# Gate/up and w_down of a hybrid encoder layer by seven block products instead of eight

## The chip, the cores and the metric

The kernel runs on one core of one Trainium2 chip. The metric is the device time of one execution in microseconds (us), as the median of several runs. In the profile PE is the tensor engine (TensorE), PEld its weight loads, DVE the vector engine (VectorE), ACT the scalar engine (ScalarE), POOL the GpSimd engine, SP the engine that only issues DMA transfers. TensorE has two clock levels, 1.2 and 2.4 GHz; the column PEclk is the granted share of the full one.

## What is computed

One layer over 512 tokens of width 2048: a token mixer (a gated recurrence beside sparse attention, merged by gates and an output projection), a residual with layer norm, and then the part that changes here:

```python
def swiglu(h, w_gate, w_up, w_down):
    return (jax.nn.silu(h @ w_gate) * (h @ w_up)) @ w_down
...
        h = x * (1.0 + sc_f) + sh_f
        y = swiglu(h, w_gate[l], w_up[l], w_down[l])
        x = layer_norm(ALPHA * x + (1.0 + gt_f) * y, ln2_g[l], ln2_b[l])
```

`w_gate` and `w_up` are 2048 x 5632, `w_down` is 5632 x 2048, all float32.

## The kernel before

Every float32 product runs as three passes in a rounded format: an operand x is split into hi, its rounded copy, and lo = x - hi, and hi*hi + hi*lo + lo*hi is accumulated in PSUM (`mm3`, whose matmuls stand at line 204 of the profile). Activations are feature-major, 128 features on the partitions and 512 tokens along the row, wherever they feed a product; `m_hi` and `m_lo` hold the 16 feature tiles of the normed h.

Weights come as one stream of 128 x 1024 tiles of 512 KB in the order of their use. `Stream.load_to` (line 285) issues the loads on SP into five raw buffers; `round_to` (line 319) rounds a tile to hi on ScalarE, `split_to` (line 331) takes lo on VectorE, into four pairs of buffers. Both run two tiles ahead of the products. The order of instructions on each engine is the order in which the program issues them.

Gate and up (`gate_up`, products at line 204 on tiles `gate` and `up`): for each of 44 feature tiles of 128, gate takes 16 feature tiles of h times three passes, 48 matmuls with all 512 tokens moving, and up as many. ScalarE takes silu of gate out of PSUM (line 1188), VectorE multiplies by up (line 1190), and the result is split (lines 246, 247). The very first feature tile is taken in two halves of 256 tokens while the last two token tiles are still being normed: `finish1` norms a token tile, transposes it (`zt`, line 1096), scales it on ScalarE (line 1103) and splits it on VectorE.

w_down (`down`, tile `dn`): after each part of four feature tiles, for each of four column blocks of 512 and each of four token tiles, 12 matmuls with 128 tokens stationary and 512 weight columns moving. VectorE multiplies each weight tile of w_down by the gate row `gtf` before it is split (line 1022), and adds each PSUM bank into the residual's accumulator (line 1209), which began as ALPHA (z g + b) (`base_side`, on GpSimd). The last part goes token tile by token tile: add (line 1265), statistics (line 1266), `ln_scale`, and `norm` (lines 1272 to 1278), which writes the output.

`Side` holds generators (`finish1`, `base_side`) that are advanced a step between slices of the large products. GpSimd's DMA queue carries the loads of x, of the merge gates and of the layer norm rows.

Of the kernel before, what the change touches and what calls it, by code (L numbers as in the profile page):

```python
# [13 lines left out]
"""  # L14
# [14 lines left out]
P = 128  # L29
# [27 lines left out]
NHEAP = 38  # L57
NSMALL = 14
# [12 lines left out]
def stream_keys():  # L71
    """The weight tiles in the order in which the products use them."""
# [28 lines left out]
    def gu(p):  # L101
        return [(g, f, i) for f in range(p * PART, p * PART + PART) for g in ("gate", "up") for i in range(2)]

    def down(p):
        return [("down", f, c) for c in range(4) for f in range(p * PART, p * PART + PART, 2)]

    ks += gu(0)
    for p in range(1, NPART):
        ks += gu(p) + down(p - 1)
# [3 lines left out]
    ks += [k for k in down(NPART - 1) if not k[2]] + stay  # L113
    return ks
# [3 lines left out]
def layer_kernel(ctx, tc, ws, wa, wada, xt, x, cin, bada, lbl, ghg, gcq, gckv, ln1c, lnrow, ident, lvm, dist, out):  # L118
# [6 lines left out]
    hp = ctx.enter_context(tc.tile_pool(name="heap", bufs=NHEAP))  # L125
# [6 lines left out]

    def big(name, dt=FR):
        return bp.tile([P, 4, T], dt, name=name, tag="big")
# [4 lines left out]
    # ---------------------------------------------------------------- constants  # L139
# [18 lines left out]
    # cond = silu(c) on every partition  # L158
# [64 lines left out]
    keys = stream_keys()  # L223
# [25 lines left out]
    class Stream:  # L249
        def __init__(self):  # L250
# [10 lines left out]
        def room(self, kind):  # L261
            """The pool that an entry is loaded into, and how many of it may be there."""
# [8 lines left out]
        def load_to(self, e):  # L271
            """Load at least up to this entry, and as far as the room reaches."""
            while self.ndma < len(entries):
                kind = entries[self.ndma]
# [1124 lines left out]
```

## Time and profile before

| | |
|---|---|
| median of 3 runs | 2917.91 us (2916.67 to 2919.34) |
| profiled execution, span of its instructions | 2914.7 us |
| what the median of the runs has beyond that span | 3.2 us |
| TensorE busy | 2874.3 us, 99% of the span |
| VectorE, ScalarE, GpSimd busy | 1664.9, 865.0, 382.3 us |
| DMA traffic | 407.46 MB, mean 140 GB/s |

The profiled execution's own time is given by its span alone, so it stands against the runs by their median. The span runs from the first to the last instruction. Engines work side by side, and their busy times are not summed.

### The profile page before, as it was taken

The page shows a single profiled execution, that of the slowest core. Times are in us where ns is not written, and L with a number is a line of the kernel's source. Part 1 is how long each engine was busy: PE and PEld are TensorE (multiplying, and loading weights), DVE is VectorE, ACT ScalarE, POOL GpSimd, SP SyncE. Part 2 cuts the span into 40 slices and gives each one's busy share as a digit, 9 for nine tenths or more (in the row PEclk, how much of TensorE's full clock was granted, in tenths as well). Part 3 has the DMA queues.
Part 4 walks back from the last instruction along what each step waited for, and adds up shares of the span by engine and source line. Part 5 has one row for each costly group of instructions (what it writes and reads, how often), then busy time and mean ns, then how long its engine had stood idle before and what let it go on. Part 6 is the DMA issues. An engine that isn't in the chain of part 4 may idle for free.

```text
span 2914.7 us, 33709 instructions
## 1 busy us (share of the span) xinstructions
PE 2874.3 (99%) x13226; PEld 2391.8 (82%) x13226; DVE 1664.9 (57%) x2429; ACT 865.0 (30%) x1276; POOL 382.3 (13%) x435
## 2 busy tenths in 40 slices
PE   8999999999999999999999999999999999999997
PEld 6878888888888888888888888888888888888885
DVE  7877777778834876456643534244343524344358
ACT  4334342333223554222332222222222222222221
POOL 1011223332012443000062000000000000000003
PEclk9999999999999999999999999999999999999998
DMA  9866455557952124444233322332332233232341
GB/s 387 329 203 190 154 170 175 177 174 261 315 194 95 51 73 169 149 137 130 75 121 101 102 96 92 101 100 88 102 100 96 93 102 99 89 101 97 105 132 65
DMA packets 116049, 407.46 MB, mean 140 GB/s; under 512 B 14225, under 2 KB 14529, under 8 KB 112817
## 3 DMA queue, kind: packets, MB, share of 16 engines
q1 hardware_dynamic: 104690, 369.35, 37.7%
q0 software_dynamic: 10912, 35.64, 3.8%
q8 instruction: 104, 1.70, 0.2%
q14 instruction: 55, 0.45, 0.1%
q10 hardware_dynamic: 288, 0.31, 0.0%
HBM read 386.62 MB, written 16.27 MB: 138 GB/s over the span
## 4 chain that ended last, share of the span: by engine, by line
PE 94%; DVE 3%; DMA 1%; issue 1%; ACT 0%; POOL 0%; SPq 0%; DVEq 0%; POOLq 0%; ACTq 0%
PE gate L204 16%; PE up L204 16%; PE dn L204 16%; PE y L204 6%; PE gb L204 6%; PE ga L204 6%; PE qb L204 3%; PE pb L204 3%; PE g L204 3%; PE v L204 3%; PE pa L204 2%; PE early L204 2%; PE s L204 2%; PE a L204 1%; PE q L204 1%; PE f L204 1%
## 5 line engine op out<-in xcount | busy, mean ns | idle before, releaser
L331 DVE TENSOR_TENSOR wlo<-raw,whi 128x1024 fp32r<-128x1024 f32 (+1 forms) x486 | 597.2, 1251 | 474.4 <-ACT whi L319 470.2
L319 ACT ACTIVATE whi<-raw 128x1024 fp32r<-128x1024 f32 (+1 forms) x486 | 498.7, 1047 | 514.0 <-DVE raw L1022 241.3
L204 PE MATMUL gate<-mhi,wlo 128*128 128x512 f32 (+1 forms) x720 | 276.8, 384 | 0.0
L204 PE MATMUL up<-mhi,wlo 128*128 128x512 f32 (+1 forms) x720 | 276.8, 384 | 0.0
L204 PE MATMUL gate<-mlo,whi 128*128 128x512 f32 (+1 forms) x720 | 276.7, 384 | 0.0
L204 PE MATMUL gate<-mhi,whi 128*128 128x512 f32 (+1 forms) x720 | 276.7, 384 | 0.0
L204 PE MATMUL up<-mlo,whi 128*128 128x512 f32 (+1 forms) x720 | 276.7, 384 | 0.0
L204 PE MATMUL up<-mhi,whi 128*128 128x512 f32 (+1 forms) x720 | 276.7, 384 | 0.0
L204 PE MATMUL dn<-whi,gthi 128*128 128x512 f32 x656 | 255.2, 389 | 0.0
L204 PE MATMUL dn<-wlo,gthi 128*128 128x512 f32 x656 | 255.2, 389 | 0.0
L204 PE MATMUL dn<-whi,gtlo 128*128 128x512 f32 x656 | 255.2, 389 | 0.0
L1209 DVE TENSOR_TENSOR t<-t,dn 128x512 f32<-128x512 f32 x160 | 106.5, 684 | 141.2 <-PE dn L204 140.2
L1190 DVE TENSOR_TENSOR silu<-silu,up 128x512 f32<-128x512 f32 x43 | 29.6, 687 | 271.3 <-PE up L204 271.3
L1253 POOL DMA_DIRECT2D l<-in_lnrow x8 | 4.3, 542 | 1299.0 <-PE dn L204 1212.4
L204 PEld LDWEIGHTS gate<-mlo,whi 128*128 128x128 f32 x720 | 135.3, 188 | 26.9
L204 PEld LDWEIGHTS gate<-mhi,whi 128*128 128x128 f32 x720 | 135.3, 188 | 26.8
L204 PEld LDWEIGHTS up<-mlo,whi 128*128 128x128 f32 x720 | 135.3, 188 | 26.8
L204 PEld LDWEIGHTS up<-mhi,whi 128*128 128x128 f32 x720 | 135.3, 188 | 26.8
L204 PEld LDWEIGHTS gate<-mhi,wlo 128*128 128x128 f32 x720 | 135.3, 188 | 26.8
L204 PEld LDWEIGHTS up<-mhi,wlo 128*128 128x128 f32 x720 | 135.3, 188 | 26.8
L204 PEld LDWEIGHTS dn<-whi,gthi 128*128 128x128 f32 x656 | 123.1, 188 | 25.6
L204 PEld LDWEIGHTS dn<-wlo,gthi 128*128 128x128 f32 x656 | 123.1, 188 | 25.6
(349 smaller groups left out, 5672.2 us busy)
## 6 DMA issues: line engine op xcount, KB each, us to landing
raw<-in_ws SPq DMA_DIRECT2D x480, 512.0 KB, 3.9
raw<-in_wada SPq DMA_DIRECT2D x128, 512.0 KB, 4.9
rawb<-in_wada SPq DMA_DIRECT2D x22, 1024.0 KB, 12.1
raws<-in_wada SPq DMA_DIRECT2D x40, 256.0 KB, 6.3
d_gate<-sgate POOLq DMA_DIRECT2D x32, 256.0 KB, 3.0
raw<-in_wa SPq DMA_DIRECT2D x16, 384.0 KB, 10.0
raws<-in_xt SPq DMA_DIRECT2D x16, 256.0 KB, 10.3
spa<-d_gate POOLq DMA_DIRECT2D x16, 256.0 KB, 3.1
```

The source lines that it names most:

```text
L204: mmul(*a, **k)
L319: nc.scalar.activation(hi, src, AF.Copy)
L331: nc.vector.tensor_sub(lo, src, hi.bitcast(FT))
L1190: nc.vector.tensor_mul(s, s, ps)
L1209: nc.vector.tensor_add(yacc[t][c], yacc[t][c], ps)
L1253: nc.gpsimd.dma_start(rows2[n][c], lnrow[2 + n][:, c * T:c * T + T].to_broadcast([P, T]))
```

## The change

The product of two matrices cut into 2 x 2 blocks is taken by seven block products instead of eight.

For gate and up the blocks of the weights are feature tiles p and p + 22 of the output (the first digit of a block's name) and the two halves of the 2048 input features (the second digit), and h is cut into the same halves of features and into two halves of 256 tokens. A group (`gu`, n) is one pair of feature tiles of gate or up; there are 44, with seven products each (p1, q7, r6, p2, q5, q4, p3). A product takes one 128 x 1024 weight block and eight feature tiles of one 256-token half of h or of a combination of halves: 24 matmuls of 256 columns. The combinations R4 to R7 of h are made once by `block_sums`, after `finish1`. The products accumulate in three PSUM banks per group; the partial sums are copied out by ScalarE and combined by VectorE.

The weights need four sums, S3 = 11 + 21, S1 = 21 + 22, S2 = S1 + 11, S4 = S2 + 12. For all but the first four groups VectorE adds them from the four loaded tiles, between three steps ahead of a group's first product and two steps behind it. For the first four groups (32 transfers, issued during the product with w_pb) and for w_down (176 transfers of 512 KB, issued during gate and up) GpSimd issues DRAM to DRAM transfers, half of them plain copies and half with an add at the destination.

For w_down the blocks are token halves, halves of the 5632 rows and halves of the 2048 columns. `give` forms seven combinations of the activations on VectorE and stores them to DRAM over SP's queue (seven stores of 128 KB for each of 22 pairs); `factor_load` and `factor_tiles` bring them back and split them, eight and four steps ahead. There are 7 x 11 x 2 products of 12 matmuls of 512 columns, summed over all rows in PSUM. The gate row and the base are applied at the end (`join`) and not to each weight tile; the base is formed during the w_down products from normed rows that were spilled to DRAM. The last four products go token tile by token tile.

Weight tiles are still 128 x 1024 in five raw buffers and four pairs, now prepared three steps ahead. The general tile pool of 38 buffers is split after the merge into one of 14 buffers and one of six larger ones; for w_down a pool of 24 stands in the latter's place. The output projection (`y`) keeps its products; its x tiles, the held tiles of w_out and the residual rows (spilled to and read back from DRAM) now pass through the six larger buffers.

The diff, cut to its core:

```diff
+    def block(g, what):
+        if what[0] == "S":
+            return d_sum[g, what]
+        i, j = int(what[0]) - 1, int(what[1]) - 1
+        if g[0] == "gu":
+            return ws[at_row[("gate", "up")[g[1] % 2], g[1] // 2 + i * NP2, j]]
+        return ws[at_row["down", 2 * g[1] + j * NP2, 2 * i + g[2]]]
...
+        return [(g, dst, src, add) for dst, src, add in (
+            ("S3", "11", False), ("S1", "21", False), ("S3", "21", True), ("S1", "22", True),
+            ("S2", "S1", False), ("S2", "11", True), ("S4", "S2", False), ("S4", "12", True)) for g in groups]
+    def add_up(g, dst, src, add):
+        nc.gpsimd.dma_start(d_sum[g, dst], block(g, src), **({"accum_op": OP.add} if add else {}))
+    first_jobs = sum_jobs([("gu", n) for n in range(NPRE)])
+    down_jobs = sum_jobs([("dn", n, cc) for n in range(NP2 // 2) for cc in range(2)])
...
+        for i in ("R7", "R6", "R5", "R4"):
+            raw = {}
+            for t in (0, 1):
+                for c in range(2):
+                    h11, h12, h21, h22 = (hraw.get(at) for at in ((t, c), (t + 2, c), (t, c + 2), (t + 2, c + 2)))
+                    if i == "R7":
+                        raw[t, c] = h22
+                        nc.vector.tensor_sub(h22, h12, h22)
...
+    first = [("gu", n) for n in range(NPRE)]
+    steps = [Unit(first[n], i) for n0 in range(0, NPRE, 2) for i in ("p1", "p2") for n in (n0, n0 + 1)]
+    steps += [Unit(g, i) for i in ("q7", "r6") for g in first]
+    steps += [Unit(g, i) for g in first for i in ("q5", "q4", "p3")]
+    for n in range(NPRE, 2 * NP2):
+        steps += [Unit(("gu", n), i) for i in SEVEN]
+    nsteps = len(steps)
+    steps += [Unit(("dn", n, cc), i) for i in SEVEN for n in range(NP2 // 2) for cc in range(2)]
...
+        for ahead, what in ((7, "11"), (6, "21"), (5, "22"), (5, "12")):
+            fetch.setdefault(s - ahead, []).append((("gu", n), what))
+        for ahead, what in ((3, "S3"), (3, "S1"), (2, "S2"), (-2, "S4")):
+            adds.setdefault(s - ahead, []).append((("gu", n), what))
...
+            fetch.setdefault(max(n - 6, -1 if n < 5 else 0), []).append((u.group, u.i))
...
+    OF = {"p1": "11", "q7": "S3", "r6": "S2", "p2": "12", "q5": "S1", "q4": "22", "p3": "S4"}
...
+            if what == "S3":
+                r = raws[g, "S3"] = new_raw()
+                add(r, raws[g, "21"], raws[g, "11"])
+            elif what == "S1":
+                r = raws[g, "S1"] = raws.pop((g, "21"))
+                add(r, r, raws[g, "22"])
+            elif what == "S2":
+                r = raws[g, "S2"] = raws.pop((g, "11"))
+                add(r, r, raws[g, "S1"])
+            else:
+                r = raws[g, "S4"] = raws.pop((g, "kept"))
+                add(r, r, raws.pop((g, "12")))
...
+        ps = acc[n, name][:, :H]
+        whi, wlo = u.pair
+        for k in range(8):
+            w = slice(k * P, k * P + P)
+            mm3(ps, whi[:, w], wlo[:, w], *factor(i, k), i in FRESH and k == 0, k == 7, f=mmul, skip_group_check=True)
+            if n < NPRE and k % 4 == 3:
+                side.step()
...
+        sub(r[:, :H], a[:, :H], a[:, H:])
+        sub(r[:, H:], a[:, H:], b[:, H:])
+        sub(q[:, :H], r[:, H:], a[:, :H])
+        nc.vector.tensor_add(q[:, H:], b[:, :H], q[:, :H])
+        for i, v in (("p1", a[:, :H]), ("q7", r[:, H:]), ("r6", q[:, :H]), ("p2", b[:, :H]), ("q5", r[:, :H]),
+                     ("q4", q[:, H:]), ("p3", b[:, H:])):
+            nc.sync.dma_start(d_r[i, p // 2][:, p % 2], v)
...
+        fresh = n == 0 and i in FRESH + ("q4",)
+        if fresh:
+            acc[at] = bank(f"dn{CHAIN[i]}")
+        for k in range(2):
+            s = slice(k * H + t * P, k * H + t * P + P)
+            w = slice(k * T, k * T + T)
+            mm3(acc[at], hi[:, s], lo[:, s], whi[:, w], wlo[:, w], fresh and k == 0,
+                n == NP2 // 2 - 1 and k == 1, f=mmul, skip_group_check=True)
...
-                ps = bank(kind)
-                for i in range(2):
-                    whi, wlo = W.get(kind, f, i)
-                    for kk in range(8):
-                        k = 8 * i + kk
-                        w = slice(kk * P, kk * P + P)
-                        mm3(ps, whi[:, w], wlo[:, w], *mh(k), k == 0, k == KD - 1)
...
-                ps = bank("dn")
-                for f, w in zip(fs, wl):
-                    down_mm(ps, t, f, f == fs[0], f == fs[-1], w)
-                nc.vector.tensor_add(yacc[t][c], yacc[t][c], ps)
...
+        nc.vector.tensor_mul(y, y if ps is None else ps, gtf[:, c * T:c * T + T])
+        nc.vector.tensor_add(y, y, base.pop((t, c)))
+        nc.vector.bn_stats(st2[t][:, c * 6:c * 6 + 6], y)
...
+        if step + 3 < len(steps):
+            prepare(step + 3)
+        fetch_behind(step)
+        for ahead, do in ((4, factor_tiles), (8, factor_load)):
+            if step + ahead < len(steps):
+                v = steps[step + ahead]
+                if v.group[0] == "dn" and v.group[2] == 0:
+                    do(v.i, v.group[1])
...
+        if step >= 20 and u.group[0] == "gu":
+            goal = (step - 20) * len(down_jobs) // (nsteps - 60)
+            while njobs < min(goal, len(down_jobs)):
+                add_up(*down_jobs[njobs])
+                njobs += 1
```

## Rows read from the trace of the kernel before

**Rows 1.** Page, busy time of engines: us, share, instructions.

```profile
PE 2874.3 (99%) x13226; PEld 2391.8 (82%) x13226; DVE 1664.9 (57%) x2429; ACT 865.0 (30%) x1276; POOL 382.3 (13%) x435
```

**Rows 2.** Page, chain that ended last, share by engine.

```profile
PE 94%; DVE 3%; DMA 1%; issue 1%; ACT 0%; POOL 0%; SPq 0%; DVEq 0%; POOLq 0%; ACTq 0%
```

**Rows 3.** Waits of PE: us in total, times, longest.

```profile
PE a L204 <- ACT hThi L436: 5.9, 1, 5.9
```

**Rows 4.** Chain in order of time: start, us, what.

```profile
1578.45 10.88 PE up L204 x48
...
1632.85 43.52 PE dn L204 x192
...
2807.89 65.29 PE dn L204 x288
```

**Rows 5.** Timeline of PE, first feature tile: start, us, what.

```profile
1455.59 0.28 PE L204 MATMUL gate<-mhi,whi 128*128 128x256 f32 x1
...
1467.74 0.28 PE L204 MATMUL up<-mhi,whi 128*128 128x256 f32 x1
...
1472.90 0.28 PE L204 MATMUL gate<-mlo,whi 128*128 128x256 f32 x1
```

**Rows 6.** Timeline of PE, last matmul.

```profile
2894.54 0.39 PE L204 MATMUL dn<-wdhi,gtlo 128*128 128x512 f32 x1
```

**Rows 7.** PE groups by form: out<-in, shape, count.

```profile
L204 PE MATMUL gate<-mhi,whi 128*128 128x512 f32 x688 | 267.6, 389 | 0.0
...
L204 PE MATMUL dn<-whi,gthi 128*128 128x512 f32 x656 | 255.2, 389 | 0.0
...
L204 PE MATMUL dn<-wdhi,gthi 128*128 128x512 f32 x48 | 18.7, 389 | 0.0
...
L204 PE MATMUL gate<-mhi,whi 128*128 128x256 f32 x32 | 9.0, 283 | 0.0
```

**Rows 8.** Windows: us, busy by engine (instructions), PEclk, DMA share, GB/s.

```profile
20.00:80.00 60.00, 58.12 (x249) 46.94 (x248) 50.90 (x58) 28.30 (x40) 6.11 (x8) 1.00 1.02 413
750.00:800.00 50.00, 50.00 (x222) 41.43 (x221) 40.62 (x64) 11.99 (x14) 3.23 (x6) 1.00 0.92 310
1500.00:2700.00 1200.00, 1200.00 (x5296) 993.65 (x5295) 489.70 (x505) 266.63 (x297) 45.96 (x30) 1.00 0.30 97
1465.00:1470.00 5.00, 5.00 (x44) 5.00 (x43) 3.13 (x6) 2.19 (x7) 1.69 (x3) 1.00 0.51 156
```

**Rows 9.** VectorE groups by form: busy us, mean ns, idle before.

```profile
L331 DVE TENSOR_TENSOR wlo<-raw,whi 128x1024 fp32r<-128x1024 f32 x470 | 582.0, 1261 | 469.4 <-ACT whi L319 465.3
...
L1022 DVE TENSOR_TENSOR raw<-raw,gtf 128x1024 f32<-128x1024 f32 x88 | 104.3, 1219 | 0.0
...
L1190 DVE TENSOR_TENSOR silu<-silu,up 128x512 f32<-128x512 f32 x43 | 29.6, 687 | 271.3 <-PE up L204 271.3
...
L690 DVE TENSOR_TENSOR ks<-kt,G 128x256 f32<-128x256 f32 x48 | 20.0, 418 | 0.0
...
L1276 DVE SCALAR_TENSOR_TENSOR t<-t,mv,l 128x512 f32<-128x512 f32 x9 | 12.9, 1434 | 0.0
```

**Rows 10.** ScalarE groups by form, same columns.

```profile
L319 ACT ACTIVATE whi<-raw 128x1024 fp32r<-128x1024 f32 x470 | 485.2, 1054 | 482.2 <-DVE raw L1022 241.3 <-PE dn L204 129.4 <-DMA raw<-in_ws 47.0
...
L1103 ACT ACTIVATE h<-zt,colB,colA 128x128 f32<-128x128 f32 x64 | 23.1, 481 | 11.1 <-PE zt L1096 11.1
...
L901 ACT ACTIVATE pthi<-t 128x256 fp32r<-128x256 f32 x16 | 6.4, 399 | 0.0
```

**Rows 11.** DMA of 1500 to 2700 us: queue share; issues, median us to landing.

```profile
q1 hardware_dynamic: 31680, 115.36, 29.5%
...
raw<-in_ws SPq DMA_DIRECT2D x220, 512.0 KB, 4.0
```

**Rows 12.** DMA of 700 to 900 us, issues on SP, same columns.

```profile
raw<-in_wada SPq DMA_DIRECT2D x39, 512.0 KB, 5.6
```

**Rows 13.** Chain in order of time, last statistics of VectorE.

```profile
2903.26 0.70 DVE sf L1266
```

More of the change, by code (lines that the diff above doesn't have):

```diff
@@ L57 @@
 NHEAP = 38
+NSTAY = 14
+NPRE = 4
 NSMALL = 14
@@ new lines, in layer_kernel, with new_raw, fetch_behind @@
+    for n, u in enumerate(steps):
+        if u.group[0] == "dn" or u.group in first:
+            fetch.setdefault(max(n - 6, -1 if n < 5 else 0), []).append((u.group, u.i))
+    OF = {"p1": "11", "q7": "S3", "r6": "S2", "p2": "12", "q5": "S1", "q4": "22", "p3": "S4"}
+    def new_raw():
+        return wp.tile([P, 1024], FT, name="raw", tag="raw", bufs=NRAW)
+    def fetch_behind(step):
+        for group, what in fetch.pop(step, ()):
+            r = raws[group, what] = new_raw()
+            nc.sync.dma_start(r, block(group, OF.get(what, what)))
@@ new lines, in add_behind @@
+    def add_behind(step):
+        add = nc.vector.tensor_add
+        for g, what in adds.pop(step, ()):
+            if what == "S3":
[7 more added lines that the diff above has]
+                add(r, r, raws[g, "S1"])
+            else:
+                r = raws[g, "S4"] = raws.pop((g, "kept"))
+                add(r, r, raws.pop((g, "12")))
@@ L1125, in layer_kernel, with prepare @@
+    def prepare(step):
+        if step >= len(steps):
+            return
+        u = steps[step]
+        g = u.group
+        r = raws.pop((g, u.i), None)
+        if r is None:
+            r = raws[g, OF[u.i]]
+            if u.i == "r6":
+                raws[g, "kept"] = r
+            if u.i not in ("p1", "p2"):
+                del raws[g, OF[u.i]]
+        u.pair = u.place() if hasattr(u, "place") else W.pair()
+        split(r, *u.pair)
     for c in range(4):
-        xs = [xin_load(t, c) for t in range(NT)]
@@ new lines, in layer_kernel, with factor_load, factor_tiles, dn_mm @@
+    facts = {}
+    part = {}
+    small = heap
+    def factor_load(i, n):
+        r = facts[i, n] = heap("raws")
+        nc.sync.dma_start(r, d_r[i, n].rearrange("p k q -> p (k q)"))
+    def factor_tiles(i, n):
+        r = facts[i, n]
+        facts[i, n] = (small("fhi", FR), small("flo", FR))
+        split(r, *facts[i, n])
+    def dn_mm(u, t):
+        (_, n, cc), i = u.group, u.i
+        whi, wlo = u.pair
+        hi, lo = facts[i, n]
+        at = CHAIN[i], cc, t
+        fresh = n == 0 and i in FRESH + ("q4",)
[6 more added lines that the diff above has]
+                n == NP2 // 2 - 1 and k == 1, f=mmul, skip_group_check=True)
@@ new lines, in layer_kernel @@
+    KEEP = 4
+    for u in steps[len(steps) - KEEP:]:
+        u.place = lambda: (lambda w: (w[:, :2].rearrange("p a b -> p (a b)"), w[:, 2:].rearrange("p a b -> p (a b)")))(big("wkeep"))
+    gtf = None
+    njobs = 0
+    for step in range(len(steps)):
+        u = steps[step]
+        if step + 3 < len(steps):
[6 more added lines that the diff above has]
+                    do(v.i, v.group[1])
+        last = step >= len(steps) - KEEP
+        if u.group[0] == "gu":
+            gu_product(u)
+            gu_use(u)
+        elif not last:
+            dn_product(u)
+            dn_use(u)
+        add_behind(step)
+        if not last:
+            u.pair = None
+        if step == 3 * NPRE + 2:
+            for t in range(NT):
+                side.drain(t)
+            assert not hraw
+            gtf = gate_row(1, "gtf")
+        if step >= 20 and u.group[0] == "gu":
[3 more added lines that the diff above has]
+                njobs += 1
+        if step == nsteps - 1:
+            del m_hi, m_lo
+            mh = None
+            sums.clear()
+            xp.release()
+            yp = ctx.enter_context(tc.tile_pool(name="tail", bufs=24, side="right", reuse_waits="tile"))
+            small = lambda name, dt=FT: yp.tile([P, T], dt, name=name, tag="y")
+            for i in "EYV":
+                part[i] = big(i, FT)
+            side.add(0, base_side())
+            side.add(1, end_side())
@@ L1299, in token_order @@
+    res = big("res", FT)
+    for t in range(2):
+        for cc in range(2):
+            for u in steps[len(steps) - KEEP:]:
+                if u.group[2] == cc:
+                    dn_mm(u, t)
+            join(t + 2, cc, res[:, 2 * cc + t], acc["V", cc, t])
+        if t == 0:
+            side.drain(0)
+            side.drain(1)
+        mv = ln_scale(st2[t + 2], "mv2")
+        for c in (2, 3, 0, 1):
+            norm(t + 2, c, mv, c < 2 if t == 0 else c == 0)
 def token_order():
```

422 lines of the change are left out of this document (262 added, 160 removed).

## The prediction

> **What bounds the kernel now.** I began with the busy times: TensorE works 2874.3 of 2914.7 us, VectorE little over half of that [rows 1]. The chain that ended last lies to 94% on TensorE [rows 2], and the longest of TensorE's waits is 5.9 us, once, in the first stage [rows 3]. So only TensorE's own work and a new wait of it count. The chain in order of time then shows the pace: 48 matmuls of 512 columns take 10.88 us, 226.7 ns each, for gate and up as for w_down, where 192 take 43.52 us [rows 4]. The clock is at its upper level (PEclk 1.00) in every stretch that I read [rows 8].
>
> The change needs the pace at 256 columns, and the first feature tile shows it: from 1467.74 to 1472.90 us there are 43 steps, 120.0 ns each [rows 5]. That is more than half of 226.7: 512 columns less 256 is 106.7 ns, and 13.3 ns are paid per matmul whatever its width. Weight loads fill that window wholly (PEld 5.00 of 5.00 us) [rows 8], so they may set the 120 ns; a matmul still narrower would gain less again.
>
> As a test of both paces: the forms give 2 x 3 x 688 matmuls of 512 columns and 2 x 3 x 32 of 256 for gate and up, 3 x (656 + 48) of 512 for w_down [rows 7]. 192 x 0.120 + 4128 x 0.2267 + 2112 x 0.2267 = 1437.4 us. From the first gate matmul at 1455.59 [rows 5] to the last of all, 2894.54 + 0.23 [rows 6], are 1439.2 us; the rest are transposes. The model closes within 2 us.
>
> **TensorE's work after.** Gate and up become 44 groups x 7 products x 24 = 7392 matmuls of 256 columns: 887.0 us against 23.0 + 935.7 = 958.7. Columns fall by an eighth, time by 7.5%, for the 13.3 ns are paid nearly twice as often. w_down becomes 154 products x 12 = 1848 of 512 columns: 418.9 against 478.7. Removed from the path: 71.7 + 59.8 = **131.5 us**.
>
> The Trainium skill, page "TensorE: Matmul & The Clock Gate", section "Back-to-back issue gap", puts the warm spacing at N/2.4 plus about 2.5 ns. As an estimate by that rule the stage before would take 1368 us and the stage after 1206, a saving of 162; the trace disagrees with the rule by about 11 ns per matmul [rows 4, 5], and I go by the trace.
>
> **VectorE under gate and up.** A group lasts 7 x 2.88 = 20.16 us on TensorE. VectorE has 7 splits of 1.261 and 4 sums of 128x1024; the gate-row multiply has that shape, 1.219 us: 13.7 us [rows 9]. A gate group adds three 256-column steps of 0.418 (1.3 us); an up group nine and one of 0.687, `give` included (4.4 us). That is 15.0 and 18.1 us, 82% on average. The heavy steps are q5, q4 and p3 of an up group, together about 11 us in 8.64; tiles are prepared three products ahead, and the next group's first products bring only a split each, so the 2 us of arrears are absorbed. ScalarE: 7 x 1.054 plus some six steps of 0.4 to 0.6 [rows 10], 11 us. I cost the sums on VectorE at nothing, hidden under the products; if that cover went (VectorE at 1.434 us per 512 columns, as beside a busy GpSimd [rows 9]), it is rival 3.
>
> **Loads and SP's queue.** Gate and up load four blocks per 20.16 us, 104 GB/s, where before carried 97 [rows 8, 11]. With the raw buffer that each takes over freed by a split or a sum, block 21 starts some 2.4 products before S3 is formed, and S3 has another product or two before its split is late: about 10 us for a load that lands in 4.0 [rows 11], 5.6 on a busy queue [rows 12]. `give`'s seven stores stand in SP's queue ahead of the next loads and wait for VectorE at the end of an up group; those loads' buffers come free at that same time, so nothing. w_down needs 512 KB and half of a 256 KB factor per product of 2.72 us, 241 GB/s, plus the base (6.3 MB over some 180 us, 35): 276 GB/s. From 750 to 800 us the core moved 310 GB/s with TensorE busy throughout [rows 8]. Nothing again, bounded by 0 and 10 us.
>
> **Adding transfers.** The trace has none, and no DRAM to DRAM copy. 176 jobs over 248 products are one per 4.06 us. A 512 KB load costs 1.27 us of the 16 DMA engines when these are full (413 GB/s [rows 8]), 1.61 by the share of the quiet stage (29.5% of 1200 us over 220 loads [rows 11]). Below, an add costs as much as a load; above there is no row, so I work out where it begins to matter. Suppose the two queues take turns and an add costs x. Then a weight load costs 1.27 + x in the add phases, and TensorE needs one per 5.04 us: no loss up to x = 3.77, then 88 adds lose 88 (x - 3.77). Two reads and a write against one of each suggest x = 2 x 1.61 = 3.2: nothing. GpSimd's queue in the earlier merge gets two jobs per 10.88 us pair of products ahead of the gates' loads; it runs ahead of TensorE, so nothing.
>
> The Trainium skill, page "Collectives: The Full Stack", section "The bandwidth ceiling", says that an adding transfer moves about half of what a copy does, because it has two sources to read. No run here shows it yet; by it the estimate for x would be about 2.5 us, and the sum stays as it is.
>
> **The way into gate and up.** Here the cover is thin. Under products 0 to 11 (34.6 us) VectorE has 12 splits (15.1), 16 combinations and 16 rests of 512 columns in `block_sums` (32 x 0.687 = 22.0 [rows 9]), six 256-column steps (2.5) and about 5 us of the last token tile: 44.6 us. ScalarE has 12 roundings (12.6), 16 of half size (about 8.4), 16 scalings of 0.481 (7.7) and 8 copies (3.2), 32 us [rows 10]. VectorE is 10 us over; three products prepared ahead cover up to 8.6 of it, but R7's and R6's roundings come late in its queue, and the splits behind them. I take 10 us lost; bounds 0 (the lead covers it) and 25 (the two engines also alternate, 16 x 0.53 = 8, and the scalings hold up R7 by 7). The output projection now reloads rows behind the store of the token tile before, under 10.88 us of matmuls: 0 to 10, nothing.
>
> **The end.** After the last matmul before has 19.9 us; its last statistics are at 2903.26 [rows 13], so VectorE lags 9 us behind. After, the two last token tiles have join (three steps of about 0.7) instead of two, four times in 10.9 us, then the same norms. -4 to +6, I take 0. The 88 multiplies by the gate row and 160 bank additions go, but they were off the path.
>
> **Sum.** Against the runs: 2917.9 - 131.5 + 10 = **2796 us**; in the span, 2793. Its own bounds: 2781 to 2815.
>
> **The rivals.**
> 1. *The way in costs 25 to 40 us*, the output projection's reloads included: 2811 to 2826. For it: VectorE's 44.6 us in 34.6. Against: before, TensorE waited for nothing there [rows 3]. Chance 0.10.
> 2. *Adds starve weight loads in part*, x between 3.8 and 5.1: at 4.5, 88 x 0.73 = 64 us lost, 2860. For: adds take most of the traffic; against: the doubling gives 3.2. Chance 0.11.
> 3. *VectorE becomes the bound* of up groups: at 1.6 us for each of the 11 large steps they take 22.0, 1.9 over, 22 times: 2838. Against: nothing but DMA issues runs on GpSimd there. Chance 0.04.
> 4. *Slower*: the adds are the bound. Place: the add phases of gate and up. Break-even is 88 (x - 3.77) = 121.5, x = 5.15, that is 3.2 loads of the quiet stage; at four loads (6.4) 231 us are lost, 3027 us. For: no row prices an add, and the 13.3 ns leave only 4.5% to lose. Against: nothing in the rows asks for more than double. Chance 0.12. The Trainium skill, page "DMA: Bandwidth & Descriptors", section "Issuing engines are not separate DMA queues", speaks for a collision: the queues of SP and GpSimd share the same 16 DMA engines. The order of the two queues is untested here.
> 5. *No change*: x between 5.09 and 5.22, or several smaller losses. Chance 0.03, of which 0.02 falls within the band.
>
> My forecast has the remaining 0.60.
>
> **How the numbers follow.** A difference of 0.2%, 6 us, is about what a measurement of this kernel can tell. Faster: 0.60 + 0.10 + 0.11 + 0.04 = 0.85; same 0.02; slower 0.13. The range begins at 2778 (no way-in loss, shorter end) and goes up to 2860: all of the forecast, rivals 1 and 3 and half of rival 2, 0.80.
>
> **What would show it.** Right: matmuls of 256 columns 120 ns apart through gate and up; TensorE idle only near 1460 to 1500 us, behind VectorE's `block_sums`; about 1316 us from first gate to last w_down matmul; VectorE at 15 to 18 us per group; every add landing in under some 5 us. Wrong: TensorE's waits naming weight tiles (`whi`, `wlo`) with SP's loads behind them during gate and up, landing times over 10 us, a slower pace at 256 columns over long stretches, or a w_down product that waits for a sum.

## The result: slower by 2.2%

| | before | changed |
|---|---|---|
| median of the runs | 2917.98 us (2916.67 to 2919.34) | 2980.89 us (2979.12 to 2981.79) |
| span of the profiled execution | 2914.7 us | 2979.7 us |

The ratio is 1.0216, interval 1.0201 to 1.023. The forecast was 2796 us, the range ended at 2860, and "slower" had a chance of 0.13: the prediction was wrong.

The page of the changed kernel, busy times, then the chain's shares by engine:

```profile
PE 2795.7 (94%) x16034; PEld 2450.3 (82%) x16034; DVE 2047.6 (69%) x2878; ACT 1162.2 (39%) x1725; POOL 567.0 (19%) x687
...
PE 72%; DMA 12%; DVE 8%; issue 4%; ACT 3%; POOL 1%; SPq 0%; DVEq 0%; ACTq 0%; POOLq 0%
```

Against [rows 1, 2], TensorE's busy time fell by 79 us, but it is no longer busy throughout: its share of the chain fell from 94 to 72%, and transfers went from 1 to 12%. Where that is, a view of stretches shows (us, busy by engine, PEclk, DMA share, GB/s):

```profile
1500.00:1560.00 60.00, 57.27 (x457) 56.86 (x457) 36.54 (x48) 29.46 (x43) 12.91 (x25) 0.94 0.86 321
1560.00:1600.00 40.00, 22.90 (x153) 22.20 (x152) 18.64 (x22) 9.76 (x13) 10.34 (x20) 0.74 1.03 374
1600.00:1700.00 100.00, 78.11 (x626) 76.70 (x626) 58.25 (x66) 33.20 (x46) 28.52 (x35) 0.91 1.06 256
1700.00:1800.00 100.00, 71.55 (x554) 70.44 (x553) 48.92 (x55) 30.11 (x42) 25.25 (x39) 0.86 1.05 304
1800.00:1900.00 100.00, 68.55 (x531) 66.96 (x531) 51.36 (x59) 27.32 (x38) 24.46 (x38) 0.86 1.05 295
1900.00:2000.00 100.00, 79.37 (x638) 77.88 (x637) 58.18 (x67) 34.31 (x48) 16.28 (x20) 0.91 0.90 227
2000.00:2500.00 500.00, 499.86 (x4196) 499.65 (x4195) 389.64 (x440) 231.13 (x317) 0.19 (x1) 1.00 0.40 132
```

From 1560 to 2000 us TensorE stands idle for a fifth to over two fifths of the time, with the DMA engines full up to 1900. From 2000 us on it is busy throughout at 119.2 ns per matmul (500 / 4196) with VectorE 78% busy: the products, the pace and the sums on VectorE are as forecast there. The difference is what GpSimd does, 10 to 29 us busy in each stretch up to 2000 us, nothing after.

The stops cost twice, for in the longer ones the granted clock falls to the lower level (1.2 GHz). The first row is within a stop of 9.9 us that ends at 1595.4. The next are gate/up as a whole, in the changed kernel and in the same kernel without w_down's sum transfers (e1 below):

```profile
1590.00:1592.00 2.00, 0.00 (x0) 0.00 (x0) 0.00 (x0) 0.00 (x0) 0.52 (x1) 0.50 1.03 399
1467.20:2501.80 1034.60, 910.25 (x7409) 902.67 (x7408) 690.82 (x795) 418.09 (x589) 118.88 (x179) 0.94 0.69 207
...
1464.50:2354.90 890.40, 884.35 (x7410) 882.69 (x7409) 690.08 (x795) 419.13 (x589) 1.61 (x3) 1.00 0.42 137
```

TensorE stands 124.4 us of the stage against 6.1, and is busy 910.3 us against 884.4 for the same matmuls. Of the 144 us between the two, 118 are standing and 26 are slower work, for after such a stop the matmuls first come 0.21 us apart instead of 0.12.

The waits of TensorE and of ScalarE (in total, times, longest), and the shares of the chain within 1540 to 1700 us:

```profile
PE V L237 <- ACT vq L1399: 95.4, 7, 16.8
...
ACT whi L272 <- DMA raw<-in_ws: 109.3, 13, 17.5
...
by line: DMA raw<-in_ws 64.8%; DVE wlo L273 13.8%; issue 7.3%; ACT whi L272 7.2%; DMA raw<-sum_gu 6.4%; DVE raw L1278 3.6%; PE V L237 1.8%; PE V L239 1.6%; PE V L238 1.6%; DVE raw L1281 1.4%; DVE act L1405 1.3%; DVE r L1424 0.8%; DVE r L142
```

TensorE's wait names `vq`, a copy out of PSUM on ScalarE. Such a copy takes about 0.4 us (386 ns in the median), so it can't be the cause of a wait of 16.8: on the same engine it stands behind a rounding (`whi`) that waits for its weight tile, and the chain says so, 64.8% of it being the landing of weight loads. The transfers of 1620 to 1700 us (queue: packets, MB, share of the 16 engines; issues, median us to landing):

```profile
q0 software_dynamic: 3709, 13.51, 84.8%
q1 hardware_dynamic: 2641, 5.86, 21.2%
...
sum_dn<-in_ws POOLq DMA_DIRECT2D x26, 512.0 KB, 24.6
raw<-in_ws SPq DMA_DIRECT2D x11, 512.0 KB, 22.8
```

A weight load lands in 22.8 us, against 4.0 before [rows 11]. GpSimd's queue (q0) has over four fifths of the engines' time (the shares of the two queues overlap and add up to more than 100%). And GpSimd is not paced by the products. Its timeline at the start and at the last job (start, us, what, idle before), and its total waits:

```profile
1512.94 3.60 POOL L1085 DMA_DIRECT2D sum_dn<-in_ws  x7
1520.69 0.52 POOL L1085 DMA_DIRECT2D sum_dn<-in_ws  x1 [4.16 <-DMA gtf<-d_row]
1523.25 0.52 POOL L1085 DMA_DIRECT2D sum_dn<-in_ws  x1 [2.04 <-DMA sum_dn<-in_ws]
...
1952.67 0.81 POOL L1085 DMA_DIRECT2D sum_dn<-in_ws  x1 [2.94 <-DMA sum_dn<-in_ws]
...
POOL sum_dn L1085 <- DMA sum_dn<-in_ws: 252.2, 119, 4.4
...
POOL sum_dn L1085 <- DMA sum_dn<-sum_dn: 52.2, 40, 2.6
```

A job waits for an earlier one to land (159 times here) and never for a product: the gate row `gtf` and seven jobs go out at once, the eighth job goes when `gtf` has landed, the ninth when the first job has, so that eight are under way at a time. All 176 are issued in 440 us, from 1512.94 to 1952.67, one per 2.5 us instead of one per 4.06.

### The profile page after: what moved, and what is told of

The parts are those of the page before. It is cut to its first block, busy times and chain, and to the rows that moved or that the text cites. A ratio compares the mean times of both kernels' runs of the same rounds, so it can differ in the third digit from the quotient of the medians.

```text
span 2979.7 us, 41496 instructions
## 1 busy us (share of the span) xinstructions
PE 2795.7 (94%) x16034; PEld 2450.3 (82%) x16034; DVE 2047.6 (69%) x2878; ACT 1162.2 (39%) x1725; POOL 567.0 (19%) x687
## 4 chain that ended last, share of the span: by engine, by line
PE 72%; DMA 12%; DVE 8%; issue 4%; ACT 3%; POOL 1%; SPq 0%; DVEq 0%; ACTq 0%; POOLq 0%
DMA raw<-in_ws 9%; PE gb L229 6%; PE y L229 6%; PE ga L229 6%; PE V L237 3%; PE V L238 3%; PE V L239 3%; PE qb L229 3%; PE pb L229 3%; PE g L229 3%; DVE wlo L273 3%; PE v L229 3%; PE pa L229 2%; PE early L229 2%; PE s L229 2%
## 5 line engine op out<-in xcount | busy, mean ns | idle before, releaser
L273 DVE TENSOR_TENSOR wlo<-raw,whi 128x1024 fp32r<-128x1024 f32 x458 | 567.9, 1252 | 348.4 <-ACT whi L272 347.4
L272 ACT ACTIVATE whi<-raw 128x1024 fp32r<-128x1024 f32 x458 | 482.2, 1058 | 603.2 <-DMA raw<-in_ws 109.3
L237 PE MATMUL V<-mhi,whi 128*128 128x256 f32 x1056 | 305.8, 290 | 95.4 <-ACT vq L1399 95.4
L359 DVE TENSOR_TENSOR wlo<-raw,whi 128x1024 fp32r<-128x1024 f32 (+1 forms) x228 | 284.5, 1251 | 112.8 <-ACT whi L347 112.0
L347 ACT ACTIVATE whi<-raw 128x1024 fp32r<-128x1024 f32 (+1 forms) x228 | 233.7, 1039 | 191.7 <-DVE raw L1050 76.9
L238 PE MATMUL V<-mlo,whi 128*128 128x256 f32 x1056 | 304.1, 288 | 0.0
L239 PE MATMUL V<-mhi,wlo 128*128 128x256 f32 x1056 | 303.9, 288 | 0.0
L238 PEld LDWEIGHTS V<-mlo,whi 128*128 128x128 f32 x1056 | 208.5, 197 | 0.0
L237 PE MATMUL Y<-R,whi 128*128 128x256 f32 x704 | 200.8, 285 | 7.3 <-ACT whi L272 7.3
L238 PE MATMUL Y<-R,whi 128*128 128x256 f32 x704 | 200.0, 284 | 0.0
L237 PEld LDWEIGHTS Y<-R,whi 128*128 128x128 f32 x704 | 135.1, 192 | 7.7 <-ACT whi L272 7.7
L238 PEld LDWEIGHTS Y<-R,whi 128*128 128x128 f32 x704 | 135.4, 192 | 0.0
```

Of the source, the lines that this page charges most:

```text
L237: f(ps, ahi, bhi, start=first, stop=False, **k)
L238: f(ps, ahi, blo, start=False, stop=False, **k)
L239: f(ps, alo, bhi, start=False, stop=last, **k)
L272: nc.scalar.activation(hi, src, AF.Copy)
L273: engine.tensor_sub(lo, src, hi.bitcast(FT))
L347: nc.scalar.activation(hi, src, AF.Copy)
```

## Experiments

My theory is that the transfers that form w_down's sums take the DMA engines from the weight loads, first because they go out as fast as they land, then because an adding one costs more than a copy. Rivals are VectorE's load, the place of the operands in the memory, and the waits at w_down's base. The table has the length of the stages in us, from the first matmul of one to the first of the next (w_down: to the end of the last matmul). It is read from each kernel's profiled execution; the last column is the median of its runs (e4: a single run). Before, gate/up and w_down are interleaved, 1439.2 together [rows 5, 6]:

| kernel | merge (pa, pb) | y | gate/up | w_down | median |
|---|---|---|---|---|---|
| before | 179.0 | 179.5 | | | 2918 |
| changed | 183.5 | 180.0 | 1034.6 | 459.5 | 2980.89 |
| e1 no sums | 183.5 | 180.1 | 890.4 | 456.4 | 2832.48 |
| e2 paced | 183.5 | 180.1 | 955.4 | 457.3 | 2901.60 |
| e4 copies | 184.2 | 180.1 | 980.0 | 458.7 | 2930.42 |
| e11 paced copies | 183.5 | 180.1 | 899.5 | 457.4 | 2849.46 |
| e3 pool moved by 96 bytes | 182.9 | 180.1 | 1033.0 | 453.8 | 2978.44 |
| e5 pool moved by 2016 bytes | 179.0 | 179.5 | 1039.2 | 454.2 | 2967.18 |
| e6 first sums later | 183.5 | 180.1 | 1035.6 | 458.5 | 2982.27 |
| e7 spread wider | 183.4 | 180.1 | 914.8 | 512.3 | 2919.96 |
| e8 four edits | 178.9 | 179.5 | 922.7 | 444.1 | 2853.10 |
| e10 blocks | 179.3 | 179.5 | 932.6 | 421.2 | 2838.01 |
| e9 no sums, base ahead | 183.5 | 180.1 | 890.9 | 439.3 | 2814.61 |
| e12 floor | 179.0 | 179.5 | 896.8 | 421.8 | 2794.08 |

**e1_no_sums**, w_down's 176 sum transfers left out:

```diff
+            if g[0] == "dn":
+                return block(g, "11")
...
-            while njobs < min(goal, len(down_jobs)):
+            while False:
```

> Leaves out all 176 transfers that form the sums for w_down; the products that need a sum load a plain weight block of the same size, so the output lacks the sums. Theory 1 (these transfers, run back to back, hold up the weight loads): gate and up take about 895 us from first to last matmul instead of 1034, the run about 2840 us. Theory 2 (the sums on VectorE or the seven products themselves are slow): gate and up stay above 1000 us and the run within 20 us of 2981.

2832.48 us (2830.82 to 2835.91), ratio 0.9711 (0.9696 to 0.9725). This is what theory 1 said. Gate/up falls by 144 us, w_down by 3. The transfers cost 148 us and turn the sign, for without them the kernel is 2.9% faster than before. The rest of the way to the forecast, 36 us, has other causes.

**e2_paced**, GpSimd goes on with the jobs due at a step only when VectorE has split the weight tile three steps ahead:

```diff
+    seen = cp.tile([P, 1], FT, name="seen")
...
+            if njobs < min(goal, len(down_jobs)):
+                tick = cp.tile([P, 1], FT, name="tick", tag="tick", bufs=15)
+                nc.vector.tensor_copy(tick, steps[step + 3].pair[1][:, :1].bitcast(FT))
+                nc.gpsimd.tensor_copy(seen, tick)
```

> All transfers stay, but GpSimd waits before each due group of jobs for a one-column copy that VectorE makes after the split three products ahead, so that the 176 jobs really go out one per 1.4 products (4.06 us). Theory 1 (GpSimd's queue ran ahead of TensorE and flooded the DMA engines): most of the 140 us come back, 2845 to 2885 us, with some waits left in the add phases, where an add takes about 2.55 us of the 16 engines. Theory 2 (an add is too dear at any pace): 2940 us or more. Cost of the pacing itself: 176 small copies, under 1 us per group on VectorE.

2901.60 us (2898.08 to 2907.57), ratio 0.9948 (0.9933 to 0.9963), between its two theories. With one job per 1.41 products, as the prediction assumed, the kernel takes 0.5% less than before. As the products themselves take longer, that is one job per 4.4 us (the first is issued at 1546.1 us, the last at 2316.4) and not 4.06. Gate/up still takes 65 us more than without sums.

**e4_copies** and **e11_paced_copies**: the 88 adding transfers as plain copies, unpaced and paced.

```diff
-        nc.gpsimd.dma_start(d_sum[g, dst], block(g, src), **({"accum_op": OP.add} if add else {}))
+        only = {"accum_op": OP.add} if add and g[0] == "gu" else {}
+        nc.gpsimd.dma_start(d_sum[g, dst], block(g, src), **only)
```

> The 88 adds among the transfers for w_down become plain copies of the same bytes, so that the output lacks the sums. Theory 1 (total DMA time of the unpaced jobs counts): the jobs are over after about 300 us instead of 470, each at about 1.7 us, and the loss shrinks in proportion or more: 2880 to 2920 us. If an add cost no more than a copy: 2981 us.

> The paced kernel (one transfer per 4.06 us of gate/up, 2902 us) with its 88 adding transfers made plain copies, so the sums hold one term only; everything else as there. Theory that what the paced kernel still loses in gate/up (955 instead of 890 us) is the longer time of the adding transfers on the DMA engines: gate/up falls to 895 to 905 us and the time to 2847 us (2838 to 2860). Rival, that any transfer on GpSimd's queue delays the weight loads as much, adding or not: 2885 to 2902 us.

Unpaced, one run of 2930.42 us, a little over its theory (2880 to 2920); paced, 2849.46 us (2847.57 to 2852.13), ratio 0.977 (0.9755 to 0.9784), as expected. What gate/up takes beyond the 890.4 of e1 makes a table of two by two:

| | unpaced | paced |
|---|---|---|
| copies and adds | 144 (changed, a job per 2.5 us) | 65 (e2, 4.4 us) |
| copies only | 90 (e4, 1.9 us) | 9 (e11, 4.1 us) |

Pacing gives back some 80 us whichever the transfers are, and copies for adds some 55, paced or not. So the larger part comes of the jobs going out unpaced, eight at a time; plain copies do harm then, too. The pacing itself costs 9 us at most, for e11 has the same one-column copies. The same 100 us (1800 to 1900) of the paced kernel, in its stretch of adds:

```profile
1800.00:1900.00 100.00, 86.61 (x687) 85.15 (x686) 64.64 (x92) 37.20 (x52) 30.18 (x40) 0.95 0.89 212
...
q0 software_dynamic: 2938, 10.66, 59.1%
q1 hardware_dynamic: 4368, 10.42, 29.3%
...
sum_dn<-in_ws POOLq DMA_DIRECT2D x20, 512.0 KB, 9.4
raw<-in_ws SPq DMA_DIRECT2D x17, 512.0 KB, 12.2
```

and with copies in their place:

```profile
1800.00:1900.00 100.00, 98.10 (x815) 97.13 (x814) 77.11 (x112) 43.35 (x61) 30.64 (x50) 1.00 0.71 249
...
q0 software_dynamic: 3359, 12.26, 35.4%
q1 hardware_dynamic: 5577, 12.48, 34.8%
...
sum_dn<-in_ws POOLq DMA_DIRECT2D x25, 512.0 KB, 7.0
raw<-in_ws SPq DMA_DIRECT2D x20, 512.0 KB, 8.1
```

Per job that is 59.1 / 20 = 2.96 us of the 16 engines for an add and 35.4 / 25 = 1.42 for a copy; from 1620 to 1700 us of the changed kernel 0.848 x 80 / 26 = 2.61 for an add. The DMA engines are not full in the paced stretch of adds (0.89), and TensorE waits all the same: a load lands there in 12.2 us, with copies in 8.1.

**e7_wide**, the paced kernel with the 176 jobs spread over 330 steps, into w_down:

```diff
-        if step >= 20 and u.group[0] == "gu":
-            goal = (step - 20) * len(down_jobs) // (nsteps - 60)
+        if step >= 7 and step + 3 < len(steps):
+            goal = (step - 6) * len(down_jobs) // 330
+            if njobs < min(goal, len(down_jobs)):
+                wait_for(steps[step + 3].pair[1])
```

(`wait_for` is e2's pair of one-column copies as a function; the VectorE copy is the tick.)

> The paced kernel of before (a group of w_down's sum transfers goes out only when VectorE has split the weight tile three steps ahead), but spread wider: the 176 transfers over 330 steps from step 6 on, into w_down's first 30 steps, about one per 5.3 to 5.4 us of gate/up instead of one per 4.06; all else is as changed. Theory that the loss in gate/up is the DMA engines' time when the transfers come closer together than the loads beside them allow: mean DMA share in gate/up falls from the 0.72 to 0.89 of the paced run to 0.6 to 0.75, TensorE is over 97 us busy of each 100 there, and the time falls from 2902 to about 2865 us (2850 to 2880). Rival, that an adding transfer costs its price wherever it is put (each one delays some load): the same 2895 to 2905 us as the paced run. Rival, that VectorE's extra copies and waits take it back: over 2902 us.

2919.96 us (2918.65 to 2925.62), ratio 1.0012 (1.0003 to 1.0022): expected 2865 (2850 to 2880), a miss. Gate/up did gain 41 us (955.4 to 914.8), but w_down lost 55. The waits of VectorE and of GpSimd from 2380 to 2620 us:

```profile
DVE base L1515 <- DMA base<-d_z: 105.2, 12, 18.3
```

```profile
POOL seen L1092 <- DVE tick L1091: 57.3, 9, 9.5
```

Each holds up the other: GpSimd waits for VectorE's tick with the next base load behind it, and VectorE waits for that base block with the next tick behind it. My pacing inside w_down made this wait longer; the changed kernel has half of it without ticks (52.3 us at the base in w_down's first 200).

**e9_base_ahead**, e1 with the base's blocks loaded one block ahead:

```diff
...
-                z = base[t, c] = small("base")
-                nc.gpsimd.dma_start(z, d_z[t, c])
+                if todo:
+                    fetch_base(*todo.pop(0))
+                for _ in range(4):
+                    yield
+                z = come.pop((t, c))
                 nc.vector.tensor_scalar(z, z, mv1[t][:, 0:1], mv1[t][:, 3:4], op0=OP.subtract, op1=OP.mult)
...
```

> The kernel without w_down's sums (its 176 sum transfers left out, the products that want a sum load block 11 instead), and with one edit more: the blocks of the second residual's base are loaded one block ahead of the VectorE instruction that takes them. Theory that the first 160 us of w_down lose about 15 us because VectorE stands at a base block that GpSimd has only just asked for, with the weight splits queued behind it: w_down takes 440 instead of 456 us, the time is 2832 - 15 = 2817 us (2812 to 2823). Rival, that these waits come from the weight loads being late, or from VectorE having too much to do there: 2828 us or more.

2814.61 us (2814.27 to 2816.05), ratio 0.9649 (0.9633 to 0.9665), as expected; w_down falls from 456.4 to 439.3. VectorE's wait from 2350 us into w_down, in e1 (to 2510 us) and then in e9 (to 2520):

```profile
DVE base L1510 <- DMA base<-d_z: 39.5, 8, 11.4
```

```profile
DVE base L1520 <- DMA base<-d_z: 1.8, 2, 1.0
```

In the changed kernel this wait shows as follows (VectorE's timeline): it stands 10.88 us at a base block, and the rests (lo) of the weight tiles and of a factor tile are queued behind it.

```profile
2517.18 0.55 DVE L1508 TENSOR_SCALAR base<-base,mv 128x512 f32<-128x512 f32 x1 [10.88 <-DMA base<-d_z]
2517.65 3.43 DVE L273 TENSOR_TENSOR wlo<-raw,whi 128x1024 fp32r<-128x1024 f32 x2
2521.00 1.76 DVE L273 TENSOR_TENSOR flo<-raws,fhi 128x512 fp32r<-128x512 f32 x1
```

**e3_aligned** and **e5_phase** ask why 512-column matmuls come more slowly in the merge and in w_down. The general pool moved to the other end of the memory; an empty pool of 96 bytes, or of 2016, puts its tiles elsewhere (24 numbers of 4 bytes in e3, as shown, 504 in e5; 376 in e8 and e10, where the ticks move the weight tiles too, and the two operands again begin at the same address modulo 2048):

```diff
+    pad = ctx.enter_context(tc.tile_pool(name="pad", bufs=1, side="right"))
+    pad.tile([P, 24], FT, name="pad", tag="pad")
     hp = tc.alloc_tile_pool(name="heap", bufs=NHEAP, side="right")
```

> An empty pool of 96 bytes ahead of the general pool moves that pool and its successors from addresses that leave 32 in division by 64 to multiples of 128; nothing else changes. Theory A (an operand that starts in the middle of 64 bytes costs each 512-column matmul 6.7 ns): matmuls with w_pa, w_pb and w_down go from 233.3 back to 226.7 ns, 768 and 1848 of them, some 17 to 25 us less: about 2960 us. Rival (the slower pace comes from the DMA traffic or from what the tiles hold): 233.3 ns stay, 2981 us.

> The changed kernel with an empty pool of 2016 bytes on the right of the memory, so that the heap's tiles begin at the same address modulo 2048 as the weight tiles (0 instead of 2016); nothing else is changed. In the traces so far the 512-column matmuls whose two operands begin at the same address modulo 512 came every 226.8 us/1000 (before: pa, pb, y and dn all at 1920 and 384; the y products of the changed kernel with both operands in the weights and the big pool at 0 and 0), and those whose operands differ came every 231.5 to 233.5 ns (changed kernel: pa, pb, part of y, all of dn; the earlier run with 96 bytes of padding: 231.5 to 232.9). Theory that the pace hangs on the two operands' addresses relative to each other: pa, pb and dn fall to 226.8 ns, the y stage begins about 4 us earlier, w_down loses 1848 x 6.5 ns = 12 us, the time is 2981 - 17 = 2964 us (2955 to 2970). Rival, that it is the place in the memory or the transfers running beside it: still 231 to 234 ns and 2975 us or more.

e3: 2978.44 us (2976.07 to 2980.31), ratio 1.0212: a miss for theory A, so alignment by itself is not it. e5: 2967.18 us (2965.67 to 2976.53), ratio 1.0177 (1.016 to 1.0193). Its pace is as expected. The chain for 24 matmuls each, in the changed kernel (233 ns), in e3 (232) and in e5 (227):

```profile
1186.54 5.60 PE pb L229 x24
```

```profile
1155.96 5.57 PE pb L231 x24
```

```profile
1185.27 5.44 PE pb L231 x24
```

The gain is 13.7 and not 17 us, in part because the 256-column matmuls go the other way, from 119.1 to 120.0 ns on average: 7392 of them give 6 us back. One row of 700 us without sums (e1, 700 / 5879), one of the floor kernel below (700 / 5836):

```profile
1600.00:2300.00 700.00, 700.00 (x5879) 700.00 (x5878) 543.78 (x611) 319.75 (x439) 0.00 (x0) 1.00 0.40 130
```

```profile
1600.00:2300.00 700.00, 700.00 (x5836) 700.00 (x5835) 538.61 (x606) 320.42 (x437) 0.00 (x0) 1.00 0.38 127
```

**e6_first_later**, the first 32 sum transfers four to every three weight tiles of the output projection:

```diff
-        for n in range(2 * j, 2 * j + 2):
-            if n < len(first_jobs):
-                add_up(*first_jobs[n])
...
+                wait_for(w[1])
+                while nfirst < (8 * c + i + 1) * len(first_jobs) // 24:
+                    add_up(*first_jobs[nfirst])
+                    nfirst += 1
```

> The 32 transfers that make the sums of the first four gate/up products are moved from the merge's products pa and pb into the first three quarters of the output projection, four in every three weight tiles, each group released by a copy of one column of the weight tile just split (VectorE, then GpSimd); all else is as changed. Theory: the 6.6 us that the changed kernel loses between 1095 and 1123 us, with weight loads landing late, come from these transfers going out all at once ahead of the products, so the y products begin about 6.5 us earlier (1280.7 instead of 1287.3) and the output projection, whose DMA share was 0.5, hides them: 2981 - 6 = 2975 us (2970 to 2979). Rival, that the loss there has another cause (the slower matmuls or the merge's own loads): 2979 to 2984 us. Rival, that the output projection can't hide them: over 2984 us.

2982.27 us (2980.54 to 2985.86), ratio 1.0223: no change, so these transfers are not what makes the merge start 6.6 us late. It starts at 1097.1 us before, 1103.7 in the changed kernel, 1100.9 in e1, 1105.8 in e6 and 1097.5 in e12. Of that, 2.4 us in the attention go with the operands' places (0 in e5 and e8); most of the rest arises in the first 200 us and differs from kernel to kernel, by a cause that was not looked for.

**e8_best** puts e5, e6, e7 and e9's base together; **e10_blocks** leaves e6's edit out, ends the jobs before w_down (292 steps, blocks of four groups) and takes the last woven norms off GpSimd:

```diff
+    down_jobs = [j for b in range(0, len(down), 4) for j in sum_jobs(down[b:b + 4])]
...
+            goal = (step - 6) * len(down_jobs) // 292
...
-                norm(t, c, mv, c % 2 == 0)
+                norm(t, c, mv, False)
```

> Four edits together: operands at the same address modulo 2048 (as in the run on the pace), the first 32 sum transfers in the output projection, w_down's 176 spread over 330 steps, and the blocks of the second residual's base loaded one block ahead of the VectorE instruction that takes them (four side steps earlier). Theory, adding what the separate edits should bring to the paced and spread kernel: 2865 - 17 (pace) - 6 (first sums) - 16 (VectorE's wait for the base and the weight splits behind it, in w_down's first 160 us) = 2826 us (2805 to 2850), under the time before by about 3%, about the run without w_down's sums (2832). Rival, that the gains overlap or one of them returns as another wait: 2850 to 2880 us.

> The best kernel so far (2853), changed in three ways: the first 32 sum transfers stand where the changed kernel has them (moving them had brought nothing); w_down's 176 transfers go out between steps 6 and 298, one per about 4.8 us and none in w_down, in blocks of four groups so that eight adds at most stand in a row (there were 44); the last norms of the woven part are VectorE's alone, without the GpSimd half that runs beside VectorE's splits. Theory that what the best kernel still loses is the stretches of adds in a row (some 28 us in gate/up) and the transfers and GpSimd work at the start of w_down (some 15 us): gate/up 905 instead of 922 us, w_down 430 instead of 444: 2825 us (2810 to 2845). Rival, that only the mean rate counts and not the order: gate/up loses more at 4.8 than at 5.3 us per transfer, 2850 us or more.

e8: 2853.10 us (2849.18 to 2857.18), ratio 0.9779 (0.9765 to 0.9794), worse than its forecast by 27 and where its rival was (2850 to 2880). e10: 2838.01 us (2836.82 to 2839.56), ratio 0.973 (0.9715 to 0.9744), the best version, 2.7% faster than before. Its sum came out within the range, its parts did not: gate/up took 932.6 and not 905, w_down 421.2 and not 430. Gate/up loses more at one job per 4.9 us than e8 at one per 5.6, as the rival said of the rate, though e10 changed the order of the jobs as well, and no run parts the two.

**e12_floor**, no sums, with e5's places, e9's base and e10's norms:

> The kernel without w_down's sums (products load block 11 instead) with three edits more: both operands of every matmul at the same address modulo 2048, the base loaded one block ahead, and the woven last norms on VectorE alone. It shows what TensorE's own work gives with the three side effects taken away. Theory by addition: 2832 - 17 (pace) - 15 (base) - 5 (norms) = 2795 us (2788 to 2806), which is the 2796 us of the prediction. Rival, that one of these returns as another wait: 2810 us or more.

2794.08 us (2793.30 to 2795.05), ratio 0.9579 (0.9565 to 0.9593). Its longest wait of TensorE is again the one of [rows 3]:

```profile
PE a L231 <- ACT hThi L466: 5.9, 1, 5.9
```

## Why the prediction was wrong

**The step that failed** is "Adding transfers", in two of its sentences.

1. "176 jobs over 248 products are one per 4.06 us." The program's `goal` only sets the order in which GpSimd's instructions stand; nothing makes that engine wait for a product, and its buffers are all in DRAM. In the prediction's own words GpSimd "runs ahead of TensorE", said there of the first 32 jobs; here it meant eight jobs at a time, one per 2.5 us. Pacing gives 79 us back (e2).
2. "No loss up to x = 3.77." An add takes 2.6 to 3.0 us, under the 3.2 that I assumed, and still costs. The bound supposed one add for each weight load, but at the pace of the other sentence there are 5.04 / 4.06 = 1.24 of them, and the bound is 3.77 / 1.24 = 3.0: the measured size stands at it, not well under it. "The two queues take turns" does not hold transfer by transfer either. From 1620 to 1700 us 26 jobs went out against 11 loads, and a load took as long to land as a job (22.8 and 24.6 us). By these times some eight jobs (26 x 24.6 / 80) and three loads (11 x 22.8 / 80) were under way, which is an estimate. By packets the queues stand closer, 3709 to 2641; what turns they take stays open.

A sum of engine time is not the whole price. In the paced stretch an add takes 2.96 us and a weight load, with what else SP's queue carries, 29.3 / 17 = 1.72; an add and its 0.81 load then ask 4.35 us in every 4.06, some 25 us over 88 adds (an estimate), and the adds cost 56 (65 less 9). There the engines are not full (0.89), and what TensorE sees is when a load lands. The prediction had the number to compare that with, "about 10 us" of cover for a block of the sums: with 12.2 us to landing TensorE is busy 87 us of 100, with 8.1 it is 98. No run changed the landing time alone, so this part is argued.

The loss in gate/up, against the kernel without sums and with its operands in the same places, is 144 us at one job per 2.5 us, 65 at 4.4, 36 at 4.9 (e10) and 26 at 5.6 (e8); with copies only it is 90 at 1.9 and 9 at 4.1. So rival 4 had the sign, but not its condition (x over 5.15), and the add phases are only part of its place: from 1560 to 1600 us the jobs are copies, and TensorE stands 17 of 40 us.

The Trainium skill, page "Collectives: The Full Stack", section "The bandwidth ceiling", says of the adding step of a collective that it runs at half the rate of a copy; these runs agree for an adding transfer (1.42 and 2.96 us in the paced pair). That rule about the size was right and did not decide. The Trainium skill, page "DMA: Bandwidth & Descriptors", section "Issuing engines are not separate DMA queues", says that the transfers of all issuing engines interleave on the same 16; here the weight loads' landing time rose to 22.8 us, which agrees. The rule on spacing that the prediction cites is, in that section of the Trainium skill's page "TensorE: Matmul & The Clock Gate", the gap of a matmul by itself; for a stream it has 131 ns at 512 columns, and the 226.7 ns of [rows 4] agrees with neither.

**What was missing**: three side effects. The places of the operands (e5) cost 6.5 ns on each 512-column matmul that takes a tile of the moved pool: 4.5 us in the merge, 0.5 in the output projection, 1848 x 6.5 = 12.0 in w_down, and 2.4 in the attention, less 6 in gate/up. In e5's own trace w_down falls by 5.3 us only (459.5 to 454.2), for there the base still holds up VectorE (55 us in its first 200). The base (e9) costs 17 us, where the prediction put w_down's loads at nothing, bounded by 0 and 10. I had said of GpSimd's queue and of SP's only what loads they carry, not that VectorE would stand at a block that GpSimd has just asked for, with the weight splits behind it. The woven norms cost w_down about 5 us by difference, for no run changed them alone: from e9 to e12 it falls by 17.5, of which the pace is 12.0.

**What held**, seen in e12, where these are gone. Gate/up is 896.8 us, 9.8 over 7392 x 0.120 = 887.0, where I took 10 for the way in:

```profile
1456.00:2352.80 896.80, 890.70 (x7409) 889.02 (x7408) 690.07 (x795) 422.23 (x590) 2.16 (x4) 1.00 0.41 136
```

Of the 9.8, TensorE stands 6.1, all between 1460 and 1520 us; the rest is work of its own, such as the 16 transposes of the last token tiles. So the 10 was close in part by luck. w_down is 421.8 against 418.9. VectorE is 77% busy in gate/up, and from 1540 us on TensorE does not wait for it, so the sums on VectorE cost nothing and rival 3 fell. The tail after the last matmul is 18.5 us in the changed kernel, 19.9 before. The sum without the transfers, 2796, is 2 us from the 2794.08 measured; its terms are off by some us each (w_down 2.9 more, the tail 1.3 less) and cancel, which is luck in part.

From e12 to the changed kernel, the span grows by 186.4 us: 6.2 up to the merge, 5.0 in merge and y, 137.8 in gate/up (144 for the transfers, less the 6 of the 256-column pace), 37.7 in w_down (base 17, places 12, norms 5, the rest 3); the tail takes the rounding.

e10 still has 36 us in gate/up over e12. Slower jobs would need a place for the rest of them; one that fills the output projection too was not tried, nor was a smaller number of jobs under way without pacing.

## What to carry to other kernels

A transfer that is issued "behind" a product in the program runs when its own engine gets there: find what that engine waits for, and if it is no product, take the transfers as issued as fast as they land (here eight at a time). Price background traffic by what it does to the landing time of the loads in the foreground against the lead that these have, and not only by whether the bytes fit. When a pool moves, read the matmul pace of a stage that the change should not touch.

## What the hardware showed that I had not expected

The spacing of matmuls hung on where their two operands begin. With both at the same address modulo 512 in the program as built (384 and 384 before, 0 and 0 in e5 and e8), 512 columns took 226.7 ns; with 480 against 0 (changed, pb and w_down), 233.3, and with 384 against 0 (e3), 232.1 in pb and 232.3 in w_down. At 256 columns it was reversed: 120.0 in e5 and e12, and 119.1 on average in e1, where three of seven products take an operand of the moved pool. Whether the same address modulo 256 is enough, and why it is so, stays open.

An adding DRAM to DRAM transfer of 512 KB took 2.6 to 3.0 us of the 16 DMA engines, a copy 1.42 in the paced kernel, and a queue with about eight of them under way got 85% of the engines' time beside a queue with about three loads.
